# A hybrid conv/attention/MoE block: the last four experts with whole weight tiles, sums begun on top of x, and stores from two queues

## The chip, the cores and the metric

One core of a Trainium2 chip runs the whole block. The metric is the device time of one execution in microseconds; the kernel before took 550.88 us (median of three runs, 549.04 to 552.13).

## What is computed

For 512 tokens of width 1024 the block does, in float32, a modulated norm, a conv group and an attention group, an output projection, and then a mixture of 32 experts (one group of four, two experts in it per token). Only that last part matters here:

```python
y = jnp.zeros_like(h)
for e in range(N_EXPERTS):
    a = jax.nn.silu(h @ w_gate_e[e]) * (h @ w_up_e[e])
    y = y + gates[:, e:e + 1] * (a @ w_down_e[e])
...
return x + g_f[:, None] * y
```

Each expert has gate and up weights of 1024 x 256 and down weights of 256 x 1024, so 3 MB in float32; all 32 have to be read once, about 100 MB.

## The kernel before

**Units.** The experts are sorted by the number of their tokens and worked off in twelve *units*: `ORDER = "eeellsllsxss"` (L921). An "e" or "l" unit holds two experts with 64 token places each, an "s" unit four experts with 32 places each, the "x" unit one with 64 and one or two pieces of 32. `PIECES` (L1011) gives the places as (first column, columns, expert). The last unit, number 11, is an "s" unit: four pieces of 32.

**Weights.** An expert's weights come as three tiles of 1 MB: part 0 and part 1 (half of the gate and half of the up rows each, two transfers of 512 KB) and "d" (down, one transfer of 1 MB). `load` (L979) takes a free place from the list `room` and returns the transfers; `loads_upto` (L1032) issues them from SP in the order of `keys`, all part 0 of a unit, then part 1, then "d". For the last unit `LAST` (L1029) changes this: its tiles are cut in two halves each, two experts at a time for parts 0 and 1 and all four at a time for "d", so that `load_keys` (L1004) issues all first halves before all second halves. The halves of "d" are column halves, 0 to 511 and 512 to 1023, as the two halves of the output are needed.

**A unit's work.** `gate_up` (L1471) multiplies the gathered tokens with gate and up (float32 products of the form 32 or 64 columns by 512; each shows as two TensorE instructions in the trace). ACT takes silu (L1483), DVE multiplies (L1485), `turn` (L1488) transposes the result on TensorE and ACT copies it to `aT` (L1494). `down` (L1496) makes, for each output half, a product per piece and per contraction half c (L1506), then DVE scales by the gate (L1509, `yf`), ACT rounds it to a first part in float32r (L1510), and POOL subtracts that to get the rest (L1511; DVE in the last unit). `one_hot` (L1460) makes on DVE the matrix that puts the rows of a unit at their tokens. `combine` (L1514) multiplies by it, for each output half and each of four blocks of 128 tokens (tt), two float32r products (L1523) into a PSUM bank, and DVE adds the bank to the rows of x in SBUF (L1526). For the last unit, `store=True`, SP then stores the 256 KB piece (L1528).

**Order.** The order of instructions on TensorE, DVE, ACT, POOL and SP is that of the program; nothing is moved by a scheduler. At the last unit (L1573 to L1589) TensorE does: the rest of the sums of the units before, `down` of unit 10, the first half of `gate_up` of unit 11, the sums of unit 10 (paced by two banks `fb` and DVE's adds), the second half of `gate_up`, `turn`, and then

```python
down, comb = cur.down(dve), combine([cur], (fb, fb, tr, tr), True)
for hf in range(2):
    run(down, 1)
    run(comb, 4)
```

so half 0 of `down`, its four sums and stores, then half 1 of `down`, its four sums and stores. PSUM has eight banks: four `acc`, two `fb`, two `tr`. After it, each engine reads the number of overflowing units (L1640) and jumps over the code for them (L1643), which is not run with these inputs.

Of the kernel before, what the change touches and what calls it, by code (L numbers as in the profile page):

```python
# [12 lines left out]
F32 = mybir.dt.float32  # L13
# [28 lines left out]
def hybrid_block(ctx: ExitStack, tc: tile.TileContext, A, out, dbg=None, stop=None):  # L42
# [52 lines left out]
    def S(shape, dt=F32):  # L95
        return slots.tile(shape, dt, tag="s", name=nm("s"))
# [49 lines left out]
    def xrow(tt):  # L146
        return X[tt // 2][:, tt % 2, :]
# [831 lines left out]
    def load(key, n):  # L979

        e, part = key
        o = Wtile()
        o.room = room.pop(0)
        shape = [128, 2, 1024] if part == "d" else [128, 2, 4, 256]
        o.t = (W if o.room == "r" else S)(shape)
        if isinstance(e, int):
            pick = lambda w: w[e]
        else:
            if part == 0:
                reg_of[e] = sp.value_load(od[0:1, e[1]:e[1] + 1], min_val=0, max_val=31)  # L990
            pick = lambda w: w[bass.ds(reg_of[e], 1)].rearrange("e p a b -> (e p) a b")
        if part == "d":
            ds = [(o.t[:, :, cs], pick(wd)[:, :, cs]) for cs in cuts(1024, n)]
        else:
            ds = [(o.t[:, k, js], pick(w)[:, 4 * part + js.start:4 * part + js.stop, :])
                  for js in cuts(4, n) for k, w in ((0, wg), (1, wu))]
        Wt[key] = o
        per = len(ds) // n
        return [ds[i:i + per] for i in range(0, len(ds), per)]
# [1 line left out]
    def cuts(m, n):  # L1001
        return [slice(i, i + m // n) for i in range(0, m, m // n)]

    def load_keys(ks):  # L1004

        for ds in zip(*[load(key, min(len(ks), 2)) for key in ks]):
            for o, i in sum(ds, []):
                sp.dma_start(o, i)


    PIECES = {2: [(0, 64, 0), (64, 64, 1)], 4: [(32 * i, 32, i) for i in range(4)],  # L1011
              "x": [(0, 64, 0), (64, 32, 0), (96, 32, 1)], 1: [(0, 64, 0)]}
# [13 lines left out]
        keys += sum(ks if units else [ks[0], ks[2], ks[1]], [])  # L1026
        units.append((kind, *u_))
    nxt = [0]
    LAST = {(units[-1][2][0], "d"): 4}  # L1029
    LAST.update({(units[-1][2][i], part): 2 for i in (0, 2) for part in (0, 1)})  # L1030

    def loads_upto(n):  # L1032
        while room and nxt[0] < min(n, len(keys)):
            m = LAST.get(keys[nxt[0]], 1)
            if len(room) < m:
                break
            load_keys(keys[nxt[0]:nxt[0] + m])
            nxt[0] += m

    dve.scalar_tensor_tensor(G2, G2, 1.0, col("nf"), op0=OP.add, op1=OP.mult)  # L1040
    dve.scalar_tensor_tensor(G2n, G2n, 1.0, col("nfn"), op0=OP.add, op1=OP.mult)
# [399 lines left out]
    class Unit:  # L1441
# [51 lines left out]
            self.aT = T()  # L1493
            act.copy(self.aT[:, :2 * n], pt[:, :2 * n])  # L1494

        def down(self, eng=pool):  # L1496

            n = self.n
            self.yhl = S([128, 2, 1024], F32R)
            for hf in range(2):  # L1500
                hs = slice(512 * hf, 512 * hf + 512)
                o = acc()
                for c in range(2):
                    for o_, w_, i in self.pieces:
                        w = self.weights(i, "d")
                        pe.matmul(o[o_:o_ + w_, :], self.aT[:, n * c + o_:n * c + o_ + w_], w.t[:, c, hs],  # L1506
                                  start=(c == 0), stop=(c == 1), tile_position=(0, o_), skip_group_check=True)
                yf = T()
                dve.scalar_tensor_tensor(yf[:n], o[:n], self.gate, gf[:n, hs], op0=OP.mult, op1=OP.mult)  # L1509
                act.copy(self.yhl[:n, 0, hs], yf[:n])  # L1510
                eng.tensor_tensor(self.yhl[:n, 1, hs], yf[:n], self.yhl[:n, 0, hs].bitcast(F32), op=OP.subtract)  # L1511
                yield

    def combine(us, banks=None, store=False):  # L1514

        for u_ in us:
            u_.one_hot()
        for hf in range(2):
            for tt in range(4):
                o = banks[tt]() if banks else fb()  # L1520
                for m, u_ in enumerate(us):
                    for k in range(2):
                        pe.matmul(o, u_.ot[:u_.n, tt * 128:(tt + 1) * 128], u_.yhl[:u_.n, k, 512 * hf:512 * hf + 512],  # L1523
                                  start=(m == 0 and k == 0), stop=(m == len(us) - 1 and k == 1))
                xr = xrow(tt)[:, 512 * hf:512 * hf + 512]
                dve.tensor_tensor(xr, xr, o, op=OP.add)  # L1526
                if store:
                    sp.dma_start(out[0, tt * 128:(tt + 1) * 128, 512 * hf:512 * hf + 512], xr)  # L1528
                yield

    def table_rows(o, reg, n):

# [38 lines left out]
    for n_ in range(len(units)):  # L1571
        last = n_ == len(units) - 1
        if last:  # L1573
            run(comb)
            run(prev.down())
            comb = combine([prev])
        cur.gate_up(lambda: last and run(comb))
        if n_ == 1:
            run(gate)
        nxt_u = start(n_ + 1)  # L1580
        if nxt_u:
            nxt_u.complete()
        if last:
            cur.turn()
            down, comb = cur.down(dve), combine([cur], (fb, fb, tr, tr), True)
            for hf in range(2):
                run(down, 1)
                run(comb, 4)
            break  # L1589
        if prev:  # L1590
            run(prev.down())
            done.append(prev)
        cur.turn()
        if len(done) == 2:
            comb, done = combine(done), []
        run(comb, 4)
        if n_ > 1:
            run(side, 1)
        r_ = [Wt[e, part].room for part in (0, 1) for e in units[n_][2]]
        if n_ < 3:  # L1600
            r_.remove("s")
        if n_:
            r_ += [Wt[e, "d"].room for e in units[n_ - 1][2]]
        room += r_
        loads_upto(len(keys))
        prev, cur = cur, nxt_u
# [4 lines left out]
    def over_body(k):  # L1611
        if k == 0:
            scatter()
        reg = sp.value_load(oi[0:1, k:k + 1], min_val=0, max_val=31)
        Wo = {}
        for part in (0, 1, "d"):
            o = Wtile()
            o.t = W([128, 2, 1024] if part == "d" else [128, 2, 4, 256])
            pick = lambda w: w[bass.ds(reg, 1)].rearrange("e p a b -> (e p) a b")
            if part == "d":  # L1620
                sp.dma_start(o.t, pick(wd))
            else:
                js = slice(4 * part, 4 * part + 4)
                sp.dma_start(o.t[:, 0], pick(wg)[:, js, :])
                sp.dma_start(o.t[:, 1], pick(wu)[:, js, :])
            Wo[part] = o
        ot_ = small(2, tag="ovt", bufs=2)
        oix = small(1, I32, tag="ovi", bufs=2)
        table_rows(ot_[:64], pool.value_load(oi[0:1, NOVER + k:NOVER + k + 1], min_val=0, max_val=NROW - 64), 64)
        dve.tensor_copy(oix[:64], ot_[:64, 0:1])  # L1630
        buf = gb[:, 0, :]
        gather(oix[:64], buf[:64], 64)
        u_ = Unit(1, ot_[:64, 0:1], ot_[:64, 1:2], buf, lambda i, part: Wo[part])
        u_.complete()
        u_.gate_up()
        u_.turn()
        run(u_.down())
        run(combine([u_]))

    n_over = nc.values_load(oi[0:1, 2 * NOVER:2 * NOVER + 1], min_val=0, max_val=NOVER)  # L1640
# [87 lines left out]
```

## Time and profile before

| | |
|---|---|
| median of three runs | 550.88 us |
| the profiled execution: device time | 550.6 us |
| its span, first to last instruction | 549.0 us |
| TensorE busy, DVE busy | 89%, 54% of the span |
| granted TensorE clock, mean | 0.968 |
| moved by DMA | 153.00 MB, 279 GB/s over the span |

In the rows further down, times are microseconds from the span's start, or nanoseconds where they say so; PE is TensorE's matmul, PEld its weight load, SPq and ACTq are the instructions that an engine's sequencer handles itself, such as the issue of a transfer. "out<-in" names tiles: `acc`, `f`, `tr` are PSUM banks, `s`, `w` the places of weights and of x, `t` the temporary tiles. A form such as 128*32 128x512 is a product with 32 stationary columns and 512 moving ones.

### The profile page before, as it was taken

The page shows a single profiled execution, that of the slowest core. Times are in us where ns is not written, and L with a number is a line of the kernel's source. Part 1 is how long each engine was busy: PE and PEld are TensorE (multiplying, and loading weights), DVE is VectorE, ACT ScalarE, POOL GpSimd, SP SyncE. Part 2 cuts the span into 40 slices and gives each one's busy share as a digit, 9 for nine tenths or more (in the row PEclk, how much of TensorE's full clock was granted, in tenths as well). Part 3 has the DMA queues.
Part 4 walks back from the last instruction along what each step waited for, and adds up shares of the span by engine and source line. Part 5 has one row for each costly group of instructions (what it writes and reads, how often), then busy time and mean ns, then how long its engine had stood idle before and what let it go on. Part 6 is the DMA issues. An engine that isn't in the chain of part 4 may idle for free.

```text
span 549.0 us, 8137 instructions
## 1 busy us (share of the span) xinstructions
PE 486.6 (89%) x2827; PEld 277.8 (51%) x2827; DVE 298.5 (54%) x631; ACT 197.3 (36%) x419; POOL 169.2 (31%) x147
## 2 busy tenths in 40 slices
PE   4999999948988979999998999999999789989962
PEld 3778865534643446688884443443434332424321
DVE  2447699998998676662456333436433231415532
ACT  4233754534578556752443513112221020211000
POOL 3110674975889563110000213112221120101100
PEclk9999999968999889999999989999999989999988
DMA  8999536935971234266959889999999999999972
GB/s 249 299 347 304 182 131 257 381 113 179 231 217 67 78 93 149 78 236 213 367 180 382 291 346 335 347 409 413 373 414 408 410 411 415 408 410 303 327 296 96
DMA packets 60946, 153.00 MB, mean 279 GB/s; under 512 B 7485, under 2 KB 27085, under 8 KB 55264
## 3 DMA queue, kind: packets, MB, share of 16 engines
q1 hardware_dynamic: 57712, 145.91, 74.7%
q0 software_dynamic: 1792, 3.97, 2.1%
q10 hardware_dynamic: 1392, 2.51, 1.3%
q8 instruction: 24, 0.39, 0.3%
q14 instruction: 26, 0.21, 0.1%
HBM read 149.84 MB, written 4.49 MB: 281 GB/s over the span
## 4 chain that ended last, share of the span: by engine, by line
PE 46%; DVE 23%; DMA 20%; ACT 3%; SPq 3%; issue 2%; POOL 1%; ACTq 0%; DVEq 0%; POOLq 0%
DVE dw L345 10%; PE acc L1480 10%; DMA s<-in_w_up_e_dram 9%; PE acc L1506 6%; PE f L1523 5%; DMA w<-in_w_up_e_dram 4%; PE acc L117 4%; PE acc L119 3%; PE acc L118 3%; DMA w<-in_w_down_e_dram 3%; DMA s<-in_w_down_e_dram 2%; DMA s<-in_w_ada_dram 2%; PE acc L909 2%; DVE sm L879 2%; PE acc L877 1%
## 5 line engine op out<-in xcount | busy, mean ns | idle before, releaser
L1480 PE MATMUL acc<-s,gw 128*32 128x512 f32 (+1 forms) x392 | 93.3, 604 | 1.5 <-DMA s<-in_w_up_e_dram 1.5
L117 PE MATMUL acc<-s,s 128*128 128x512 f32 (+3 forms) x160 | 64.8, 405 | 10.7 <-DVE s L318 8.2
L345 DVE SCALAR_TENSOR_TENSOR dw<-s,cwh,dw 128x512 f32<-128x512 f32 x60 | 63.6, 1061 | 1.5
L119 PE MATMUL acc<-s,s 128*128 128x512 f32 (+3 forms) x160 | 60.1, 376 | 1.4 <-DVE s L379 1.4
L118 PE MATMUL acc<-s,s 128*128 128x512 f32 (+3 forms) x160 | 60.1, 376 | 0.0
L1523 PE MATMUL f<-s,t 128*128 128x512 f32 x184 | 48.7, 412 | 10.8 <-DVE t L1462 8.1
L1480 PE MATMUL acc<-w,gw 128*32 128x512 f32 (+1 forms) x136 | 53.5, 619 | 4.1 <-DMA w<-in_w_up_e_dram 4.0
L1485 DVE TENSOR_TENSOR t<-t,acc 128x256 f32<-128x256 f32 x12 | 5.1, 421 | 91.0 <-ACT t L1483 91.0
L1511 POOL TENSOR_TENSOR s<-t,s 128x512 fp32r<-128x512 f32 x22 | 28.5, 1295 | 75.9 <-ACT s L1510 75.9
L1483 ACT ACTIVATE t<-acc 128x256 f32<-128x256 f32 x12 | 4.6, 384 | 127.8 <-PE acc L1480 127.8
L1480 PEld LDWEIGHTS acc<-s,gw 128*32 128x32 f32 (+1 forms) x392 | 25.8, 123 | 47.9 <-issue 46.4
L357 POOL TENSOR_TENSOR dw<-dw,s 128x512 f32<-128x512 f32 x30 | 45.6, 1518 | 13.1 <-ACT s L355 11.4
L1526 DVE TENSOR_TENSOR s<-s,f 128x512 f32<-128x512 f32 x52 | 35.2, 687 | 20.0 <-PE f L1523 20.0
L1506 PE MATMUL acc<-s,t 128*32 128x512 f32 (+1 forms) x200 | 45.3, 609 | 0.5 <-ACT t L1494 0.5
L1523 PEld LDWEIGHTS f<-s,t 128*128 128x128 f32 x184 | 31.1, 188 | 26.9 <-DVE s L1526 7.3
L1438 POOL DMA_INDIRECT s<-xg,sidx x11 | 11.2, 1020 | 106.9 <-PE tr L1454 65.5
L117 PEld LDWEIGHTS acc<-s,s 128*128 128x128 f32 x160 | 31.1, 194 | 25.2 <-DVE s L318 8.6
L1510 ACT CAST s<-t 128x512 fp32r<-128x512 f32 x24 | 14.8, 618 | 54.8 <-DVE t L1509 54.8
L119 PEld LDWEIGHTS acc<-s,s 128*128 128x128 f32 x160 | 31.1, 194 | 5.9 <-DVE s L379 1.8
L118 PEld LDWEIGHTS acc<-s,s 128*128 128x128 f32 x160 | 31.2, 195 | 3.4 <-issue 0.2
L1509 DVE SCALAR_TENSOR_TENSOR t<-acc,rt,gw 128x512 f32<-128x512 f32 x24 | 18.0, 751 | 27.0 <-PE acc L1506 27.0
L881 ACT ACTIVATE t<-acc,sm,qs 128x128 f32<-128x128 f32 (+3 forms) x32 | 19.7, 616 | 19.9 <-DVE sm L879 16.6
(313 smaller groups left out, 856.1 us busy)
## 6 DMA issues: line engine op xcount, KB each, us to landing
s<-in_w_down_e_dram SPq DMA_DIRECT2D x21, 1024.0 KB
s<-in_w_gate_e_dram SPq DMA_DIRECT2D x41, 512.0 KB
s<-in_w_up_e_dram SPq DMA_DIRECT2D x41, 512.0 KB
w<-in_w_ada_dram SPq DMA_DIRECT2D x16, 1024.0 KB
w<-in_w_gate_e_dram SPq DMA_DIRECT2D x15, 512.0 KB
w<-in_w_up_e_dram SPq DMA_DIRECT2D x15, 512.0 KB
w<-in_w_down_e_dram SPq DMA_DIRECT2D x7, 1024.0 KB
s<-in_w_ada_dram SPq DMA_DIRECT2D x6, 1024.0 KB
```

The costliest lines, as they stand in the source:

```text
L117: pe.matmul(o, lh, rh, start=start, stop=False)
L118: pe.matmul(o, lh, rl, start=False, stop=False)
L119: pe.matmul(o, ll, rh, start=False, stop=stop)
L345: dve.scalar_tensor_tensor(dw[:, t, :], u[:, t, k:k + 512], w, dw[:, t, :], op0=OP.mult, op1=OP.add)
L357: pool.tensor_tensor(dw[:, t, :], dw[:, t, :], z[(k - 1) % 2], op=OP.add)
L881: act.activation(e[:, :n], p[:, :n], AF.Exp, scale=qs[:, qt, h:h + 1], bias=H["nb"][:, qt:qt + 1], accum_out=H["rs"][:, qt:qt + 1])
L1480: pe.matmul(gu[sl, :], self.hg[:, j, sl], w.t[:, :, j % 4, :], start=(j == 0), stop=(j == 7), tile_position=(0, o_), skip_group_check=True)
L1506: pe.matmul(o[o_:o_ + w_, :], self.aT[:, n * c + o_:n * c + o_ + w_], w.t[:, c, hs], start=(c == 0), stop=(c == 1), tile_position=(0, o_), ...
L1509: dve.scalar_tensor_tensor(yf[:n], o[:n], self.gate, gf[:n, hs], op0=OP.mult, op1=OP.mult)
L1511: eng.tensor_tensor(self.yhl[:n, 1, hs], yf[:n], self.yhl[:n, 0, hs].bitcast(F32), op=OP.subtract)
L1523: pe.matmul(o, u_.ot[:u_.n, tt * 128:(tt + 1) * 128], u_.yhl[:u_.n, k, 512 * hf:512 * hf + 512], start=(m == 0 and k == 0), stop=(m == len ...
L1526: dve.tensor_tensor(xr, xr, o, op=OP.add)
```

## The change

1. The loads of the last unit: no more halves, two transfers of 512 KB for part 0 and 1 and one of 1 MB for "d", expert after expert, as in the other units. Only the very last tile ("d" of the fourth expert) comes in two column halves.
2. `down` takes both `acc` banks at its start and can work by groups of pieces. In the last unit it makes, for experts 0 and 1, both output halves, and then, for experts 2 and 3, half 0 (with DVE's scaling, ACT's rounding, and the subtraction on POOL) and half 1 (the subtraction on DVE).
3. `finish_last` replaces `down` and `combine` of the last unit. The one-hot matrix is made first. Then six of the eight sums are begun with x itself: a float32 product of the identity matrix and the rows of x, 128*128 128x512, into banks `fb`, `fb`, `tr`, `tr` for the four blocks of half 0 and `acc`, `acc` for blocks 0 and 1 of half 1. After `down` the two one-hot products go on top, and the bank is copied to SBUF: blocks 0 and 2 of half 0 on DVE, the other four on ACT. Blocks 2 and 3 of half 1 are done as before, in `fb` with DVE's add, ahead of blocks 0 and 1.
4. Stores are issued from SP and from ACT in turn.
5. `down` and `combine` are plain calls for the other units, with the same instructions in the same order.

```diff
-    LAST = {(units[-1][2][0], "d"): 4}
-    LAST.update({(units[-1][2][i], part): 2 for i in (0, 2) for part in (0, 1)})
+    LAST = units[-1][2][-1], "d"
     def loads_upto(n):
         while room and nxt[0] < min(n, len(keys)):
-            m = LAST.get(keys[nxt[0]], 1)
-            if len(room) < m:
-                break
-            load_keys(keys[nxt[0]:nxt[0] + m])
-            nxt[0] += m
+            key = keys[nxt[0]]
+            for o, i in sum(load(key, 2 if key == LAST else 1), []):
+                sp.dma_start(o, i)
+            nxt[0] += 1
...
-        def down(self, eng=pool):
+        def down(self, groups=None, first=None):
             n = self.n
             self.yhl = S([128, 2, 1024], F32R)
+            o = [acc(), acc()]
+
+            def products(hf, pieces):
+                for c in range(2):
+                    for o_, w_, i in pieces:
+                        w = self.weights(i, "d")
+                        pe.matmul(o[hf][o_:o_ + w_, :], self.aT[:, n * c + o_:n * c + o_ + w_], w.t[:, c, 512 * hf:512 * hf + 512],
+                                  start=(c == 0), stop=(c == 1), tile_position=(0, o_), skip_group_check=True)
+
+            groups = groups or [self.pieces]
+            for g in groups[:-1]:
+                for hf in range(2):
+                    products(hf, g)
             for hf in range(2):
                 hs = slice(512 * hf, 512 * hf + 512)
...
+                products(hf, groups[-1])
                 yf = T()
-                dve.scalar_tensor_tensor(yf[:n], o[:n], self.gate, gf[:n, hs], op0=OP.mult, op1=OP.mult)
+                dve.scalar_tensor_tensor(yf[:n], o[hf][:n], self.gate, gf[:n, hs], op0=OP.mult, op1=OP.mult)
                 act.copy(self.yhl[:n, 0, hs], yf[:n])
-                eng.tensor_tensor(self.yhl[:n, 1, hs], yf[:n], self.yhl[:n, 0, hs].bitcast(F32), op=OP.subtract)
-                yield
+                (dve if len(groups) > 1 and hf else pool).tensor_tensor(
+                    self.yhl[:n, 1, hs], yf[:n], self.yhl[:n, 0, hs].bitcast(F32), op=OP.subtract)
...
+    def finish_last(u_):
+
+        u_.one_hot()
+        o = {}
+        for tt, hf, bank in (0, 0, fb), (1, 0, fb), (2, 0, tr), (3, 0, tr), (0, 1, acc), (1, 1, acc):
+            o[tt, hf] = bank()
+            pe.matmul(o[tt, hf], ident, xrow(tt)[:, 512 * hf:512 * hf + 512], start=True, stop=False, skip_group_check=True)
+        u_.down([u_.pieces[:2], u_.pieces[2:]])
+        for hf, tts in (0, range(4)), (1, (2, 3, 0, 1)):
+            for n, tt in enumerate(tts):
+                xr = xrow(tt)[:, 512 * hf:512 * hf + 512]
+                known = (tt, hf) in o
+                if not known:
+                    o[tt, hf] = fb()
+                scattered(o[tt, hf], [u_], tt, hf, not known)
+                if not known:
+                    dve.tensor_tensor(xr, xr, o[tt, hf], op=OP.add)
+                elif hf or n % 2:
+                    act.copy(xr, o[tt, hf])
+                else:
+                    dve.tensor_copy(xr, o[tt, hf])
+                (act if n % 2 else sp).dma_start(out[0, tt * 128:(tt + 1) * 128, 512 * hf:512 * hf + 512], xr)
...
             cur.turn()
-            down, comb = cur.down(dve), combine([cur], (fb, fb, tr, tr), True)
-            for hf in range(2):
-                run(down, 1)
-                run(comb, 4)
+            finish_last(cur)
             break
```

`scattered` holds the two one-hot products of `combine` as they were.

## Rows read from the trace of the kernel before

**Rows 1.** The page, part 1: busy time of each engine.

```profile
PE 486.6 (89%) x2827; PEld 277.8 (51%) x2827; DVE 298.5 (54%) x631; ACT 197.3 (36%) x419; POOL 169.2 (31%) x147
```

**Rows 2.** The chain of waits in order of time, from 475 us: start, duration, what.

```profile
475.26 10.12 DMA w<-in_w_up_e_dram
...
520.27 3.64 PE acc L1480 x32
...
524.41 0.43 DVE t L1485
...
524.89 0.45 PE tr L1492 x2
...
525.78 1.97 PE acc L1506 x16
...
530.45 1.31 PE f L1523 x4
...
533.46 2.58 PE acc L1506 x16
...
538.32 0.52 PE f L1523
...
541.09 0.26 DVE s L1526
```

**Rows 3.** Waits from 470 us to the end: waiter, releaser, total, times, longest.

```profile
PE acc L1480 <- DMA w<-in_w_up_e_dram: 1.5, 1, 1.5
```

**Rows 4.** Stretches: length, busy time of PE, PEld, DVE, ACT, POOL, clock, DMA share, GB/s.

```profile
530.00:531.30 1.30, 0.85 (x4) 0.75 (x5) 0.41 (x2) 0.00 (x0) 0.00 (x0) 1.00 0.05 17
...
482.00:490.00 8.00, 6.48 (x52) 2.29 (x44) 0.38 (x1) 0.59 (x2) 0.00 (x0) 1.00 1.02 420
500.00:512.00 12.00, 12.00 (x75) 6.36 (x77) 7.16 (x11) 0.75 (x2) 2.10 (x2) 1.00 0.98 325
524.00:530.00 6.00, 2.36 (x18) 0.62 (x18) 1.96 (x4) 1.36 (x3) 0.00 (x0) 1.00 1.01 376
```

**Rows 5.** Timeline of PE at 285 us: L1236, float32, 128*128 128x512.

```profile
285.36 1.98 PE L1236 MATMUL acc<-s,rt 128*128 128x512 f32 x4
```

**Rows 6.** Timeline of PE in the "x" unit: two 32-column pieces, then 64 columns.

```profile
455.81 0.62 PE L1480 MATMUL acc<-w,gw 128*32 128x512 f32 x1
456.26 0.59 PE L1480 MATMUL acc<-s,gw 128*32 128x512 f32 x1
456.27 0.59 PE L1480 MATMUL acc<-w,gw 128*32 128x512 f32 x1
456.79 0.64 PE L1480 MATMUL acc<-s,gw 128*64 128x512 f32 x1
```

**Rows 7.** The granted clock of one stretch, columns as in rows 4.

```profile
531.34:534.76 3.42, 3.42 (x14) 1.49 (x16) 2.52 (x4) 0.00 (x0) 0.00 (x0) 0.50 0.58 214
```

**Rows 8.** Page, part 5: busy time and mean ns, idle time before; work on outputs.

```profile
L1511 POOL TENSOR_TENSOR s<-t,s 128x512 fp32r<-128x512 f32 x22 | 28.5, 1295 | 75.9 <-ACT s L1510 75.9
...
L1526 DVE TENSOR_TENSOR s<-s,f 128x512 f32<-128x512 f32 x52 | 35.2, 687 | 20.0 <-PE f L1523 20.0
...
L1510 ACT CAST s<-t 128x512 fp32r<-128x512 f32 x24 | 14.8, 618 | 54.8 <-DVE t L1509 54.8
...
L1509 DVE SCALAR_TENSOR_TENSOR t<-acc,rt,gw 128x512 f32<-128x512 f32 x24 | 18.0, 751 | 27.0 <-PE acc L1506 27.0
```

**Rows 9.** Single lines: count, ns shortest/median/longest, first and last start. PSUM to SBUF copies.

```profile
L1360 DVE COPY s<-acc x1: 691/691/691, 298.5 to 298.5; 128x512 f32<-128x512 f32 x1
...
L1359 ACT COPY s<-acc x1: 585/585/585, 297.6 to 297.6; 128x512 f32<-128x512 f32 x1
```

**Rows 10.** Single lines, same columns: issue of stores, and SP's next instruction.

```profile
L1528 SPq DMA_DIRECT2D out_dram<-s x8: 332/352/1465, 531.9 to 542.2; - x8
...
L1165 ACTq DMA_DIRECT2D xg<-t x8: 326/326/356, 268.6 to 295.0; - x8
...
L1640 SPq TENSOR_LOAD <-oi x1: 399/399/399, 543.1 to 543.1; - x1
```

More of the change, by code (lines that the diff above doesn't have):

```diff
@@ L1002, in cuts @@
         return [slice(i, i + m // n) for i in range(0, m, m // n)]
[L1004 to L1008, printed above, removed]
     PIECES = {2: [(0, 64, 0), (64, 64, 1)], 4: [(32 * i, 32, i) for i in range(4)],
@@ L1494, in turn, with scattered, combine @@
             act.copy(self.aT[:, :2 * n], pt[:, :2 * n])
-        def down(self, eng=pool):
+        def down(self, groups=None, first=None):
             n = self.n
             self.yhl = S([128, 2, 1024], F32R)
+            o = [acc(), acc()]
[9 more added lines that the diff above has]
+                    products(hf, g)
             for hf in range(2):
                 hs = slice(512 * hf, 512 * hf + 512)
[L1502 to L1507, printed above, removed]
+                products(hf, groups[-1])
                 yf = T()
-                dve.scalar_tensor_tensor(yf[:n], o[:n], self.gate, gf[:n, hs], op0=OP.mult, op1=OP.mult)
+                dve.scalar_tensor_tensor(yf[:n], o[hf][:n], self.gate, gf[:n, hs], op0=OP.mult, op1=OP.mult)
                 act.copy(self.yhl[:n, 0, hs], yf[:n])
-                eng.tensor_tensor(self.yhl[:n, 1, hs], yf[:n], self.yhl[:n, 0, hs].bitcast(F32), op=OP.subtract)
-                yield
-    def combine(us, banks=None, store=False):
+                (dve if len(groups) > 1 and hf else pool).tensor_tensor(
+                    self.yhl[:n, 1, hs], yf[:n], self.yhl[:n, 0, hs].bitcast(F32), op=OP.subtract)
+    def scattered(o, us, tt, hf, start=True):
+        for m, u_ in enumerate(us):
+            for k in range(2):
+                pe.matmul(o, u_.ot[:u_.n, tt * 128:(tt + 1) * 128], u_.yhl[:u_.n, k, 512 * hf:512 * hf + 512],
+                          start=(start and m == 0 and k == 0), stop=(m == len(us) - 1 and k == 1), skip_group_check=True)
+    def combine(us):
         for u_ in us:
@@ L1519, in combine @@
             for tt in range(4):
[L1520 to L1524, printed above, removed]
+                o = fb()
+                scattered(o, us, tt, hf)
                 xr = xrow(tt)[:, 512 * hf:512 * hf + 512]
                 dve.tensor_tensor(xr, xr, o, op=OP.add)
-                if store:
-                    sp.dma_start(out[0, tt * 128:(tt + 1) * 128, 512 * hf:512 * hf + 512], xr)
                 yield
+    def finish_last(u_):
[19 more added lines that the diff above has]
+                (act if n % 2 else sp).dma_start(out[0, tt * 128:(tt + 1) * 128, 512 * hf:512 * hf + 512], xr)
     def table_rows(o, reg, n):
@@ L1574, in hybrid_block @@
             run(comb)
-            run(prev.down())
+            prev.down()
             comb = combine([prev])
@@ L1584, in hybrid_block @@
             cur.turn()
-            down, comb = cur.down(dve), combine([cur], (fb, fb, tr, tr), True)
-            for hf in range(2):
-                run(down, 1)
-                run(comb, 4)
+            finish_last(cur)
             break
         if prev:
-            run(prev.down())
+            prev.down()
             done.append(prev)
@@ L1636, in over_body @@
         u_.turn()
-        run(u_.down())
+        u_.down()
         run(combine([u_]))
```

## The prediction

> **What bounds the kernel now.** The page's busy times come first: TensorE is busy for 89% of the span [rows 1], but that is a mean over stages, and the change touches only the last one. So the chain of waits in order of time is read next. Its last transfer is an up-weight tile of unit 10, waited for until 485.4 us; from there to the end the chain holds TensorE, DVE and ACT alone [rows 2]. The list of waits says the same: from 470 us on, products waited for a transfer once, 1.5 us, and that is the wait at 485 [rows 3]. So the weights of the last unit are not what is waited for, although they are still on their way. The stretches show how close they are: with whole tiles the queue moves 420 GB/s, with the 256 KB halves of the last unit 325 GB/s, with the halves of "d" 376 GB/s, and at 530 us it stops [rows 4]. From 524 to 530 us run some 2.26 MB; the last four 512 KB halves are 2.1 MB, so the first halves of "d" have landed at about 524.4 and the last part 1 tiles, 2.1 MB further back, at about 519. They are used at 525.78 and 520.27 [rows 2]. The transfers are 1.3 us ahead of TensorE. The reader is to see in the chain that what sets the end from 524 us on is a row of dependent steps, gone through twice: half of `down` (1.97, then 2.58 us), DVE, ACT, DVE, sums, stores.
>
> **The change part by part.** *Whole tiles.* 12.6 MB at 420 instead of 325 to 376 GB/s: begun at about 495 us, when unit 10's "d" tiles are in, they end at 495 + 30 = 525 instead of 530 us, the slow last tile included. TensorE does not wait for them before, so this gains nothing by itself; it only makes sure that "d" is there. Fewer issues on SP (21 instead of 40) gain nothing either, since SP waits for earlier transfers in any case.
>
> *Sums on top of x.* Six float32 products 128*128 128x512, two instructions each. The price of one: four such in a row take 1.98 us [rows 5], the last of them 0.6 to its end, so 0.46 between starts; the 32 of `gate_up`, four abreast and so eight steps, take 3.64 us [rows 2], 0.43 a step. I take 0.43, with 0.46 as the other end. Twelve make 5.2 us. They stand on TensorE's queue between `turn` (ends 524.89 + 0.45 = 525.34 [rows 2]) and `down`, which could start at 525.78. So 0.4 us of them lies beside ACT's copy and 4.7 us delays `down`. This is the dearest edit. It buys that six adds on DVE become plain copies, of which four go to ACT: 0.69 for DVE's add [rows 8] against 0.69 for a copy on DVE and 0.585 on ACT [rows 9].
>
> *`down` in two groups.* Before, four pieces of 32 columns ran abreast, four steps a half. Now two run abreast, twice as many steps: 4 halves of groups x 4 steps x 0.43 = 6.9 us instead of 3.4. That two of 32 run abreast is seen in the "x" unit [rows 6]. There a 64-column product waits at 456.79 until the pair begun at 456.27 is through (0.43 and 0.09), though it uses other columns; products of one size do overlap, as the four of `down`. Group 2 follows group 1 at one size, so I let its first step run beside group 1's last, 0.43 less; the other end is no overlap. The Trainium skill, "TensorEngine Tiling (Array Packing)", section Key Properties, says that different tiles run in parallel and that a change of the tiling mode drains the engine; by its rule both what rows 6 show and the overlap follow, and without the overlap the sum would be 0.4 us more.
>
> *The path.* Products with x until 530.5; group 1 until 533.9; half 0 of group 2 until 535.2, its last instruction ends at 535.4; half 1 at 537.1. Half 0 then takes DVE 0.75, ACT 0.62, POOL 1.30 [rows 8], so it is ready at 538.1, POOL's extra 0.6 us over DVE hidden half by half 1 of `down`. Half 1: 537.1 + 0.75 + 0.62 + 0.69 = 539.2 with the hops. The one-hot matrix, 0.4 us on the path before (between 529.9 and 530.45), is made while TensorE turns: gain 0.4, in the path above already. Then DVE's order counts: it does half 1's subtraction first and only then copies block 0 of half 0, until 539.95. That frees the bank for block 2 of half 1: two products to 540.6, add to 541.35, the second add (block 3) to 542.1. ACT's order counts too: the store of block 3 stands before its last two copies, waits for that add, is issued (0.33 [rows 10], and 0.1), and the copies end at 543.1 and 543.7. SP's last store goes out from 543.15 to 543.5, ACT's until 544.1. Before, the last add ended at 541.35 [rows 2], but SP's last store was issued at 542.2 and SP's next instruction began at 543.1 [rows 10], because two issues at the end took far longer than 0.35 us (the longest 1.47). From there to the end of the span 5.9 us pass, in SP's jump over the unused code and the closing of the program. They are kept, and the stores' landing lies inside them; ACT's store, 0.6 us later, has the same cover. So the span ends at 543.5 + 5.9 = 549.4, against 549.0.
>
> *Edits at nothing.* `down` and `combine` of the other units issue the same instructions in the same order. Both `acc` banks at the start of `down`: four banks, the last users are done by 524.8. Stores of half 0: issued at 532 to 534 before, beside work; now eight stores, 2 MB, fall into 539.8 to 544.1, and at the 0.32 to 0.42 MB a microsecond of rows 4 they land by 546 to 547, inside SP's 5.9 us. If that cover were gone they would cost up to 1 us.
>
> *The sum.* Against the steps of before: products with x +5.2, less the 0.4 that TensorE stood there; `down` 6.6 instead of 1.97 + 2.58, +2.0; the wait for half 0's DVE, ACT, DVE and one-hot (527.75 to 530.45) -2.7; half 0's sums between the halves (530.45 to 533.46) -3.0; from the end of `down` to the last copy that SP stores 6.0 instead of 5.3, +0.7; SP's slow issues (541.35 to 543.06, against 0.35) -1.4. Together +0.4 us. The profiled execution took 550.6 us (span 549.0, 1.6 around it), 0.3 below the median of 550.88; the median plus 0.4 is 551.3.
>
> **The clock.** From 531.34 to 534.76 the granted clock is 0.50, 1.2 GHz [rows 7], after TensorE had stood for 2.7 us; half 1 of `down` takes 2.58 instead of 1.97 us there [rows 2], the sums before it some 0.6 more. In my path TensorE is busy from 525 to 537, so I take 2.4 GHz throughout. The Trainium skill, "TensorE: Matmul & The Clock Gate", section Part 1, says that the throttled clock is the default and that activity lifts it; by its rule the fall goes, as in my sum, and were it to stay it would cost 1.7 us.
>
> **The rivals.**
> (a) *The transfers set the pace after all.* In ordinary runs they may be a little later than in this profile, only 1.3 us lie between, and TensorE would wait for the halves. Then ending 5 us earlier brings the stage forward by up to 4.4 us: 546.5. Against it: the list of waits has no such wait, and the new order puts 5.2 us of products ahead of `down`, which takes back such a gain.
> (b) *ACT stalls at its stores.* On SP one issue took 1.47 us instead of 0.33 [rows 10]. ACT has three issues ahead of its last two copies, and they would hold the copies, where SP's held nothing but stores. Stalls of 1.13 us at all three, less 1.0 us that ACT waits anyway for block 3, give +2.4: 553.7, slower. It decides from two stalls on. Against it: ACT's eight earlier stores took 0.33 to 0.36 each.
> (c) *The clock falls in `down` as before*: 3.4 us at half speed, +1.7: 553.0.
> (d) *The second queue takes away the tail's slow issues and the copies are in time*: 541.5 + 0.35 + 5.9, a span of 547.8, 549.6 for the median. For it: half of the stores leave SP. Against it: the last copies come later than the last add did.
> That the change doesn't do what it says can't be excluded for one part: products with x may wait for banks. Their last users are done by 521 (`fb`) and 525.74 (`tr`), so I give it nothing of its own.
>
> **How the numbers follow.** Half a percent, 2.75 us, is about what a measurement of this kernel can tell from no change; the three runs alone lie 3.1 us apart. The forecast has 0.58, (a) 0.10, (b) 0.14, (c) 0.08, (d) 0.10. All of (a) lies below 548.1, and 0.03 of the rest: faster 0.13. About 0.10 of (b), 0.03 of (c) and 0.05 of the forecast (no overlap, 0.46 a step, stores not covered, together 1.8 us, and noise) lie above 553.6: slower 0.18. The same 0.69. The range leaves out (a), and above it part of (b): 549.0 to 554.0.
>
> **What would show it.** Right: no wait of TensorE for transfers after 485 us; twelve instructions of some 0.43 us each between `turn` and `down`; loads at an end by 525 us; `down` over at about 537; the last copy on ACT at 543 to 544; a full clock from 525 to 540. Wrong: TensorE waiting for "d" tiles; products with x at a quarter or twice the price; store issues of over 1 us on ACT; an end more than 6.5 us after SP's last store.

## The result, and the profile after

The kernel after takes 553.04 us (median of 20 runs, 549.7 to 556.49) against 551.28 us before (20 runs, 546.95 to 553.31): ratio 1.0051 [1.003, 1.0072]. It is slower by half a percent, some 1.8 us. 551.3 was forecast, with no change as the likeliest case, at 0.69, and slower at 0.18. The value lies inside the range, but the kernel is clearly slower, and that was not the forecast.

The profiled execution has a span of 551.2 us, against 549.0 of before. First TensorE's order in the last unit, in the trace's timeline of after: start, duration, engine, line, operation, and in brackets how long the engine had stood and for what.

```profile
525.20 0.44 PE L1484 MATMUL tr<-ident,t 128*128 128x128 f32 x2 [1.04 <-DVE t L1477]
525.48 1.88 PE L1539 MATMUL f<-s,ident 128*128 128x512 f32 x4
...
530.72 0.62 PE L1498 MATMUL acc<-s,t 128*32 128x512 f32 x1
...
532.47 0.59 PE L1498 MATMUL acc<-w,t 128*32 128x512 f32 x1
532.48 1.01 PE L1498 MATMUL acc<-s,t 128*32 128x512 f32 x3
...
533.79 2.31 PE L1498 MATMUL acc<-s,t 128*32 128x512 f32 x10
...
537.36 0.96 PE L1518 MATMUL f<-s,t 128*128 128x512 f32 x3 [0.83 <-POOL s L1511]
```

The unit's `turn` starts at 525.20, 0.3 us later than before [rows 2]. The twelve instructions of the products with x follow it without a gap until `down` starts at 530.72. `down` steps every 0.43 us with two pieces abreast; from 532.47 on four are abreast, since half 0 of group 2 has joined half 1 of group 1. It is through at 536.1. Then one-hot products wait once for POOL, 0.83 us.

The engines that end the work, from the timelines of DVE, ACT and POOL of the same kernel:

```profile
536.04 1.27 POOL L1511 TENSOR_TENSOR s<-t,s 128x512 fp32r<-128x512 f32 x1 [21.89 <-ACT s L1510]
```
```profile
537.66 0.69 DVE L1511 TENSOR_TENSOR s<-t,s 128x512 fp32r<-128x512 f32 x1 [0.69 <-ACT s L1510]
538.27 0.68 DVE L1553 COPY s<-f 128x512 f32<-128x512 f32 x1
538.87 0.68 DVE L1553 COPY s<-tr 128x512 f32<-128x512 f32 x1
539.77 1.28 DVE L1549 TENSOR_TENSOR s<-s,f 128x512 f32<-128x512 f32 x2 [0.22 <-PE f L1518]
```
```profile
541.47 1.07 ACT L1551 COPY s<-acc 128x512 f32<-128x512 f32 x2 [1.49 <-PE acc L1518]
542.57 1.20 ACTq L1554 DMA_DIRECT2D out_dram<-s  x1
```

The last two copies on ACT are over at 542.54. Its last store takes 1.20 us to issue, and then ACT too has to go through the jump over the unused code. SP's four stores, in the view of line 1554 (shortest, median and longest in ns; first and last start in us):

```profile
L1554 SPq DMA_DIRECT2D out_dram<-s x4: 332/348/358, 539.0 to 542.1; - x4
```

None of SP's issues is slow any more; before, one took 1465 ns [rows 10]. So SP's last store is issued by 542.41, where before it was 543.06. Counted from the start of `turn`, 17.20 us instead of 18.18: up to here the change gains 1.0 us in these two profiles. What comes behind on SP takes the gain and more. Three views of after show it: SP's read of the register at L1662 (L1640 before, 399 ns [rows 10]), the wait at its jump, and the closing code.

```profile
L1662 SPq TENSOR_LOAD <-oi x1: 911/911/911, 542.5 to 542.5; - x1
```
```profile
SPq L1665 <- SPq L1665: 4.0, 1, 4.0
```
```profile
L1746 SPq EVENT_SEMAPHORE  x14: 17/28/28, 548.4 to 551.2; - x14
```

The jump and the closing code of before:

```profile
SPq L1643 <- SPq L1643: 2.8, 1, 2.8
```
```profile
L1724 SPq EVENT_SEMAPHORE  x14: 17/28/28, 547.4 to 548.9; - x14
```

The register read is 0.51 us longer, the jump 1.17 us (3.97 against 2.80), and the closing's fourteen semaphore instructions stretch over 2.7 instead of 1.5 us, because SP stands for 1.15 us in the middle of them. The read, the jump and the stand make 2.83 of the 2.89 us by which the stretch from SP's last store to the end has grown, 8.82 against 5.93. Less the 1.0 us won ahead of it, that is +1.9 us from `turn` to the end, about the difference of the medians.

Stretches of after, TensorE's clock and GB/s last: the loads, and the window of rows 7.

```profile
500.00:512.00 12.00, 12.00 (x76) 6.47 (x78) 6.87 (x10) 0.73 (x2) 2.10 (x2) 1.00 1.03 410
...
525.00:526.00 1.00, 0.80 (x4) 0.56 (x5) 0.55 (x2) 0.32 (x1) 0.00 (x0) 1.00 0.13 47
```
```profile
531.34:534.76 3.42, 3.42 (x27) 1.04 (x24) 0.27 (x1) 0.00 (x0) 0.00 (x0) 1.00 0.00 0
```

Whole tiles run at 410 instead of 325 GB/s [rows 4] and are in shortly after 525 instead of 530 us; TensorE waits for a transfer once after 470 us, at 485 as before [rows 3]:

```profile
PE acc L1472 <- DMA w<-in_w_up_e_dram: 1.6, 1, 1.6
```

The granted clock is 1.00 where it was 0.50 [rows 7].

### The profile page after: what moved, and what is told of

It reads as the page before. It is cut to its first block, busy times and chain, and to the rows that moved or that the text cites. A ratio compares the mean times of both kernels' runs of the same rounds, so it can differ in the third digit from the quotient of the medians.

```text
span 551.2 us, 8095 instructions
## 1 busy us (share of the span) xinstructions
PE 492.4 (89%) x2839; PEld 279.7 (51%) x2839; DVE 294.7 (53%) x626; ACT 199.2 (36%) x423; POOL 170.5 (31%) x148
## 3 DMA queue, kind: packets, MB, share of 16 engines
q0 software_dynamic: 1792, 3.97, 2.2%
## 5 line engine op out<-in xcount | busy, mean ns | idle before, releaser
L1511 POOL TENSOR_TENSOR s<-t,s 128x512 fp32r<-128x512 f32 x23 | 29.7, 1293 | 98.7 <-ACT s L1510 88.8
L1530 DVE TENSOR_TENSOR s<-s,f 128x512 f32<-128x512 f32 x48 | 32.6, 687 | 18.6 <-PE f L1518 18.6
```

Of the source, the lines that this page charges most:

```text
L1511: (dve if len(groups) > 1 and hf else pool).tensor_tensor(self.yhl[:n, 1, hs], yf[:n], self.yhl[:n, 0, hs].bitcast(F32), op=OP.subtract)
```

## The experiments

The theory to be tested: SP's tail, from its last store to the end, grew, not the engines' work. Three causes could be behind it. The stores: more of them, from two queues, are in flight when SP jumps. ACT: it now stores last and jumps at the same moment as SP. The place of the closing code: SP's program has another length, so another piece of it has to be fetched at the end. The rival to all three: the engines' new order or the whole tiles cost the time, and the tail is chance. Another is that SP simply waits for the last store to land.

One execution varies by 1.8 us (standard deviation of the twenty runs of before, and of after), so totals tell 2 us apart with difficulty; the profiles are therefore cut at two places, the start of the last unit's `turn` and the end of SP's last store issue, and the pieces compared. All in us, from one profile of each: "rest" is from the end of SP's last store issue to the end of the span, "read" SP's register read, "jump" the time from SP's branch to its next instruction, "ACT's jump" when it starts against SP's, and "stop" a stand of over 1 us between two instructions of the closing code.

| | ratio to before [95%] | turn to SP's last store | rest | read | jump | ACT's jump | stop | turn to end |
|---|---|---|---|---|---|---|---|---|
| before | | 18.18 | 5.93 | 0.40 | 2.80 | -6.4 | none | 24.11 |
| after | 1.0051 [1.003, 1.0072] | 17.20 | 8.82 | 0.91 | 3.97 | +0.95 | 1.15 | 26.02 |
| after, again (k) | 1.0031 [0.9998, 1.0064] | 17.25 | 8.83 | 0.93 | 3.90 | +0.63 | 1.22 | 26.08 |
| a | 1.0035 [1.0003, 1.0068] | 18.07 | 7.90 | 0.43 | 2.75 | -6.3 | 1.98 | 25.97 |
| b | 1.0059 [1.0018, 1.0101] | 19.71 | 5.96 | 0.60 | 2.62 | -8.1 | none | 25.67 |
| c | 1.0002 [0.9961, 1.0043] | 17.23 | 7.80 | 0.29 | 3.58 | +0.60 | 1.13 | 25.03 |
| d | 1.0029 [0.9997, 1.006] | 15.44 | 8.57 | 0.91 | 3.75 | +0.82 | 1.13 | 24.01 |
| f | 1.0000 [0.9964, 1.0037] | 17.20 | 7.56 | 0.93 | 3.90 | +0.84 | none | 24.77 |
| g | 1.0012 [0.9981, 1.0044] | 16.41 | 6.36 | 0.57 | 3.05 | -6.4 | none | 22.77 |
| h | 1.0024 [0.9998, 1.0051] | 19.31 | 6.38 | 0.54 | 3.11 | -3.1 | none | 25.69 |
| j | 1.0018 [0.999, 1.0046] | 17.45 | 6.10 | 0.62 | 2.75 | -5.9 | none | 23.56 |
| i | 0.9908 [0.9871, 0.9945] | 12.44 | 5.58 | 0.28 | 2.56 | -2.5 | none | 18.02 |
| i, again (l) | 0.9922 [0.9886, 0.9958] | 12.44 | 6.41 | 0.29 | 3.39 | -2.5 | none | 18.85 |
| m | 0.9922 [0.9884, 0.996] | 12.97 | 5.94 | 0.28 | 2.92 | -7.6 | none | 18.91 |

**a: whole tiles alone.** The kernel before with after's load code.

```diff
-    LAST = {(units[-1][2][0], "d"): 4}
-    LAST.update({(units[-1][2][i], part): 2 for i in (0, 2) for part in (0, 1)})
+    LAST = units[-1][2][-1], "d"
```

> The kernel before with the change's loads alone (whole tiles, the very last in two halves); the work on the engines, the sums and the stores stay as before. Theory 1 (the transfers were never waited for; the loss of the change is its tail, where all eight stores are in flight while the engines jump to the closing code): loads end at 525 instead of 530 us, the span stays within 1 us of before (549.0), ratio 1.000 within 0.003, and from SP's last store issue to the end of the span about 5.9 us as before. Theory 2 (the tail is longer because SP's code is shorter and lies elsewhere): from SP's last store issue to the end 7.5 us or more, time +1.5 to +2.5 us. Rival (a) of the prediction (transfers set the pace): 2 to 4 us faster.

It ran 1.0035 [1.0003, 1.0068], and not by its engines: from `turn` to SP's last store it needs 18.07 us, as before. But its closing code stops too, for 1.98 us, earlier than in after: here behind the fifth of the 26 instructions that the trace shows after SP's jump, in after behind the thirteenth. The first nine of them, which took 0.6 us after, take 2.6:

```profile
L1641 SPq EVENT_SEMAPHORE  x9: 17/17/17, 550.6 to 553.2; - x9
```

This speaks for the third cause: on the engines nothing changed, and SP's program has other loads and another length.

**b: late stores.** The kernel before; half 0's four stores are held back and issued behind those of half 1.

```diff
-                    sp.dma_start(out[0, tt * 128:(tt + 1) * 128, 512 * hf:512 * hf + 512], xr)
+                    late.append((out[0, tt * 128:(tt + 1) * 128, 512 * hf:512 * hf + 512], xr))
+                    for o_, x_ in (late[-1:] if hf else []) + (late[:4] if hf and tt == 3 else []):
+                        sp.dma_start(o_, x_)
```

> The kernel before, with the four stores of half 0 held back on SP's queue until the four of half 1 are issued; nothing else moves. The engines' work must end as before, at 541.3 us. SP issues four more stores at the end, at 0.35 to 0.6 us each: last issue 1.5 to 2.5 us later than before. Theory 1 (stores in flight delay the code of the jump): from SP's last issue to the end of the span 8 us or more instead of 5.9, so the span is 4 to 5 us longer. Theory 2 (place of the code): 5.9 us as before, the span only 1.5 to 2.5 us longer.

All eight stores now go out between 539.4 and 544.5 us, and the read, the jump and the closing stay short:

```profile
SPq L1647 <- SPq L1647: 2.6, 1, 2.6
```

The kernel is slower; its last issue comes 1.5 us later, and the rest behind it is 5.96, as before. Stores in flight didn't lengthen SP's tail here. Nor does SP wait for them to land: its first instruction behind the jump runs at 548.14, and the last store lands at 548.25. In a and in the second profile of after (k) it runs 0.17 and 0.13 us ahead of the last landing as well.

**c: half of the stores.** The kernel after, with a condition at the store.

```diff
+                if hf:
-                (act if n % 2 else sp).dma_start(...)
+                    (act if n % 2 else sp).dma_start(...)
```

> The changed kernel without the four stores of half 0 (columns 0 to 511 of the output are left out). The engines' work stays as in the changed kernel, but SP and ACT issue two stores each. Theory 1: from SP's last store issue to the end about 6 us instead of 8.8, the span 548 to 549 us, 2 to 3 us below the changed kernel and no longer than before. Theory 2: from SP's last issue to the end 8 us or more still, time within 1 us of the changed kernel.

With only four stores the jump is still 3.58 and the stop still there, 1.13; the read alone falls to 0.29. So the number of stores in flight doesn't make the jump long either; the read may depend on it. The times, 1.0002, are those of before, as if the stores had been the cause; the profile has 25.03 us from `turn` to the end, 1.0 less than after, 0.6 of it the read. SP's program is two stores shorter, and the stop has moved from behind the thirteenth of the closing instructions to behind the seventeenth.

**d: one group.** The kernel after, all four pieces abreast in `down`.

```diff
-        u_.down([u_.pieces[:2], u_.pieces[2:]])
+        u_.down([[], u_.pieces])
```

> The changed kernel with all four experts of the last unit in one group, four abreast, both halves of down one after the other; products with x, copies and stores as in the change. In the change down took 5.4 us (530.7 to 536.1), since half 1 of group 1 and half 0 of group 2 ran abreast; in one group it should take 3.5, half 0 ready 1.9 us earlier and half 1 1.9 us earlier. All theories of the tail: the whole end shifts, stores and all, span 549.3, 1.9 us below the changed kernel. If the loads were what group 2 waits for, nothing is gained (they end at 525 us, so I don't expect it).

`down` takes eight steps instead of twelve, from 531.33 to 534.9. SP's last store is issued 1.8 us sooner after `turn` than in after (15.44 against 17.20): this is what the groups cost. The tail is that of after. As no product waits for "d", nothing stands against that price. The times, 1.0029, don't tell it from after.

**f: another place.** The kernel after with 28 more stores in code that SP jumps over. They are never executed; the closing code only stands further on in SP's program.

```diff
-                    sp.dma_start(out[0, tt * 128:(tt + 1) * 128, :], xrow(tt))
+                    for cs in cuts(1024, 8):
+                        sp.dma_start(out[0, tt * 128:(tt + 1) * 128, cs], xrow(tt)[:, cs])
```

> The changed kernel with 28 more store instructions in SP's code that is jumped over (the whole rows stored in eighths), so that SP's closing code lies 29 instructions further on; nothing that is executed differs. In the changed kernel SP stands for 1.15 us between the 13th and the 14th of its 27 closing instructions, in the kernel with the loads alone, whose SP code is 8 instructions longer, for 1.98 us between the 5th and the 6th: the same place in the code. Theory 2 (place of SP's code): that stop is gone, the span 1.1 us shorter than the changed kernel's, some 550.1. Theory 1 (stores in flight), already unlikely: nothing changes.

To SP's last store it is the kernel after to the hundredth, 17.20. The stop is gone, the jump is as long as before it:

```profile
SPq L1665 <- SPq L1665: 3.9, 1, 3.9
```
```profile
L1747 SPq EVENT_SEMAPHORE  x14: 17/28/28, 549.4 to 551.0; - x14
```

Fourteen semaphore instructions in 1.6 us again, from `turn` to the end 24.77 instead of 26.02: 1.25 us less, nearly all of it the stop. The ratio of its runs is 1.0000 [0.9964, 1.0037]; the intervals of after overlap with it, so that it is the profiles that show the gain.

**g: the same for a.** The load change alone, with the same skipped stores.

> The kernel before with the change's loads alone and the same 28 instructions in SP's skipped code. Theory 2: the stop of 1.98 us in the closing code is gone, from SP's last store issue to the end 5.9 us as before, and the ratio to the kernel before is 1.000 within 0.003: whole tiles by themselves cost and gain nothing. If the loads themselves cost something, the ratio stays at 1.003 to 1.004 and the engines' work before the closing code is longer.

No stop, ratio 1.0012 [0.9981, 1.0044]. Within that interval the whole tiles neither cost nor gain anything.

That g needs only 16.41 us to SP's last store is the clock. TensorE stands as long as before, 2.74 us, but here the granted clock doesn't fall behind it, in the window that corresponds to that of rows 7:

```profile
531.32 1.17 PE L1521 MATMUL f<-s,t 128*128 128x512 f32 x4 [2.74 <-DVE t L1460]
```
```profile
532.21:535.63 3.42, 3.07 (x22) 1.06 (x20) 2.52 (x5) 0.00 (x0) 0.00 (x0) 1.00 0.60 223
```

DVE's last add ends 14.88 us after the start of `turn`; in before, a, b and j, where the clock falls to 0.50 (1.2 GHz), it is 16.43 to 16.46. So the same work takes 1.6 us more or less with the clock. Against g, the 17.20 us of after are not 1.0 us gained but 0.8 lost.

**h: one queue.** f, with all eight stores on SP.

```diff
-                (act if n % 2 else sp).dma_start(...)
+                sp.dma_start(...)
```

> The changed kernel with the 28 skipped instructions and all eight stores from SP. Compared with the kernel that has the skipped instructions and both queues. Theory 4 (the jump of SP takes 4.0 us instead of 2.8 because ACT, which now copies and stores to the very end, jumps in the same microsecond, or because two queues of stores are ahead of the code): with one queue SP's jump takes 2.8 to 3.2 us; SP's last issue comes 0.5 to 1 us later, since it has all eight; the span within 0.7 us. If the jump stays at 4 us, the second queue is not what lengthens it.

ACT is done early and jumps 3.1 us before SP. The read is 0.54, the jump 3.11, the rest 6.38 instead of 7.56: 1.2 us less. But the issues of SP are slow again, in the view of its stores:

```profile
L1554 SPq DMA_DIRECT2D out_dram<-s x8: 355/418/1444, 537.0 to 542.1; - x8
```

Its last store is issued 19.31 us after `turn`, 2.1 us later than in f, and not 0.5 to 1 us as expected. By the profiles the second queue gains 2.1 us ahead of the tail and gives 1.2 back in it; by the times the two kernels can't be told apart. Of the 1.2 us, the jump's 0.8 is no more than what two profiles of one kernel differ by (i and l, 2.56 and 3.39).

**i: what the readings point to.** Skipped stores as in f, whole tiles, one group, no product with x ahead of `down`. Only two sums are begun with x, in gaps of TensorE behind `down`, and they are ACT's, copy and store; DVE adds the other six, and SP stores them.

```diff
...
+        u_.down([[], u_.pieces])
+        begin(3, 0, tr)
+        end(3, 0)
+        end(0, 0, fb)
+        end(1, 0, fb)
+        end(2, 0, tr)
+        begin(0, 1, acc)
+        end(0, 1)
+        end(1, 1, acc)
+        end(2, 1, fb)
+        end(3, 1, fb)
...
```

`begin` makes the product with x; `end` makes the one-hot products, then the copy or the add, and the store.

> A version meant to beat both: whole tiles, one group of four abreast, both halves of down one after the other, and only two of the eight sums begun on x, each put where TensorE stands or has time (after down, and between the sums of the halves); ACT copies and stores these two, DVE adds the other six and SP stores them; SP's skipped code as in the two kernels above. From the rows of the change: turn ends at 525.4, down at 529.3, half 0's rest ready at 530.6 and half 1's at 531.6, eight sums of 0.46 us with one product of 0.86 between until 535, six adds of 0.69 us on DVE from 531.6 to 535.7, last store issued at 536.2; with 6 to 8 us behind it the span is 542 to 544.5 us, ratio 0.988 to 0.993 to the kernel before. If the stores in flight set the end (2 MB in 532 to 537.5) it is no worse than 545.

0.9908 [0.9871, 0.9945], faster than both kernels. The timelines of TensorE and DVE, first and last rows of the stage:

```profile
525.26 0.62 PE L1498 MATMUL acc<-s,t 128*32 128x512 f32 x1 [0.46 <-ACT t L1486]
...
528.31 0.60 PE L1498 MATMUL acc<-s,t 128*32 128x512 f32 x2
528.84 1.12 PE L1540 MATMUL tr<-s,ident 128*128 128x512 f32 x2
```
```profile
527.26 0.75 DVE L1509 SCALAR_TENSOR_TENSOR t<-acc,rt,gw 128x512 f32<-128x512 f32 x1 [2.55 <-PE acc L1498]
...
534.45 1.28 DVE L1551 TENSOR_TENSOR s<-s,f 128x512 f32<-128x512 f32 x2
```

Both halves of `down` run in one go from 525.26 to 528.8; they start 0.9 us behind the start of `turn`, where after starts them 5.5 us behind it. DVE's last add ends at 535.73, where before it ended at 541.35 [rows 2]. The read is 0.28, the jump 2.56, the rest 5.58.

**j, k, l, m.** The kernel before with 81 more SP instructions among those skipped, the kernel after word for word, i word for word, and i without any product with x.

> The kernel before with 81 more instructions in SP's skipped code (the whole rows stored once more in sixteenths), so that the place where the changed kernel stops lies behind the 14th of SP's closing instructions; nothing that is executed differs. Theory 2 (place of SP's code): SP stands there for 1 to 2 us, where the kernel before stood nowhere; the span 1 to 2 us longer for the same work, ratio 1.002 to 1.004. If the stop has to do with the change's loads or stores: no stop, ratio 1.000.

> The changed kernel once more, word for word, beside the others on one chip. Ratio 1.003 to 1.007 as on record; the same stop of 1.1 us in SP's closing code and a jump of SP of about 4 us, so that the rest behind SP's last store is again 8.8 us within 0.5.

> The version meant to beat both once more, beside the version without sums on x: ratio 0.987 to 0.995, span 6 to 7 us below the kernel before when the stages ahead of the last unit take the same time.

> That version without any sum on x: all eight sums added on DVE, all eight stores from SP. TensorE is 1.7 us shorter, but DVE has 8 x 0.69 us instead of 6 behind 531.6: the last add 1.4 us later, at 537.1, the last store of SP with it; ACT is done early, so SP's jump takes 2.6 to 3 us as in that version. If sums on x pay where TensorE has time: 1 to 1.5 us longer than that version. If they don't: the same within 0.5 us.

k repeats after: 17.25, 8.83, a jump of 3.90, a stop of 1.22. What the profile of after showed was no chance of one execution. l repeats i at 0.9922 [0.9886, 0.9958]. Its span is 4.8 us below before's, and not 6 to 7 as expected. Its jump is longer than i's, 3.39 against 2.56, though ACT jumps as early, so 0.8 us of SP's jump come and go in one and the same kernel. m gives the same ratio as l with no product with x at all: DVE does two adds, 1.1 us, more and waits 0.8 us less. j is a miss. The program was lengthened so that a stop should fall behind the fourteenth closing instruction, and there is none; its rest is 6.10. That place is not the one at which the others stop, but 128 instructions further on; that the stop would come again after 128 was a guess.

## Why the prediction was wrong

**The step that failed** is "From there to the end of the span 5.9 us pass, in SP's jump over the unused code and the closing of the program. They are kept". They are 8.82 (8.83 in k). The list of what would prove it wrong names it: "an end more than 6.5 us after SP's last store". The prediction kept 5.93 us because nothing in that code was edited. But its length changed with what surrounds it:

- *The stop, 1.15 us.* Shown by f, which differs from after by code that never runs and loses the stop and little else; g does the same to a. SP's program as built has 1252 instructions after (in k and d too), 1248 in c and 1260 in a, and the stop falls behind the 13th, the 17th and the 5th of the 26 that the traces show after the jump: behind the 1238th or 1239th of the program each time. In the nine profiles without a stop the program has 1281 to 1379, and that place lies in skipped code. What SP stands for is not shown. The trace has fetches of instructions, on a queue of its own kind; the view of DMA from 548 to 550 us of after lists two 8 KB packets, which start at 548.28 and 548.50, just ahead of the stop (548.66 to 549.80), and nothing else:

```profile
q14 instruction: 2, 0.02, 2.8%
```

  f has two such packets in its closing code as well, and stands nowhere. What j adds is that a place 128 instructions further on was met without a stop; whether the stop comes again at another step stays open.
- *The jump, +1.17 us.* In five profiles ACT starts its jump 0.6 to 1.0 us behind SP's, and SP's takes 3.58 to 3.97. In nine ACT starts its own 2.5 us or more ahead of SP, and SP's takes 2.56 to 3.39. The branches of after, SP's and ACT's:

```profile
L1665 SPq COMPARE_BRANCH  x1: 53/53/53, 543.7 to 543.7; - x1
```
```profile
L1665 ACTq COMPARE_BRANCH  x1: 54/54/54, 544.7 to 544.7; - x1
```

  ACT's own jump goes the same way: 3.2 to 3.7 us in the five, 3.2 and 3.3 in i and l, where DVE jumps 0.7 us behind ACT, and 2.4 to 2.7 in the other seven. b and c speak against the number of stores in flight: eight late stores with 2.62, four with 3.58. h changes only who stores, and goes from 3.90 to 3.11, which alone is within what i and l differ by. That the code of engines that jump together comes through the same fetch is the likely reading, not a shown one. The Trainium skill, "Runtime: NRT & Kernel Launch", section Instruction fetch mechanics, says that a taken branch to code outside the pages held forces a fetch before the engine goes on, and that block boundaries are mostly hidden. The jumps agree with the first: the branch itself takes 53 ns, and 2.56 to 3.97 us pass behind it. On the second, if the stop is such a boundary, 1.13 to 1.98 us of it were not hidden.
- *The read, +0.51 us.* It is 0.91 to 0.93 in the four profiles in which both queues issue all eight stores, 0.28 to 0.62 in the others. Why is open.

**The engines' path** came out better than forecast: SP's last issue ends at 542.41 instead of 543.5, though the stage began 0.3 us later. By its terms:

- *Products with x, +5.2 us until 530.5.* `down` starts at 530.72, 0.3 us of it the later start. Right. That they are the dearest edit fits d and i: where they go (and two of them return behind `down`), SP's last store comes 3.0 us sooner after `turn`, though i has another order of sums and stores, too.
- *`down` 6.6 us, over at 537.1.* It took 5.4 us, over at 536.1. The mechanism was right and the size too small: one step was allowed to overlap, but all four steps of half 0 of group 2 run beside half 1 of group 1. The Trainium skill, "TensorEngine Tiling (Array Packing)", section Key Properties, has tiles work independently; the row at 532.48 agrees, and the sum by its rule alone, twelve steps of 0.43 or 5.2 us, would have been the better one.
- *Half 0 ready at 538.1, last copy at 543.7.* POOL is through at 537.31, ACT's last copy at 542.54, 0.8 and 1.2 us earlier, about what `down` gained.
- *SP's slow issues gone, -1.4.* Right: none above 0.36 us after (0.44 in k); one returns when SP stores alone (h, 1.44).
- *ACT's last store, "the same cover".* It took 1.20 instead of 0.33 us. That issue costs nothing itself, since k, where it took 0.58, has the same rest; that ACT, busy to the end, jumps with SP was not seen.
- *Whole tiles at nothing, loads over at 525.* Right (g: 1.0012 [0.9981, 1.0044]).
- *The clock at 2.4 GHz throughout.* Right, 1.00 in the window of rows 7 and from 525 to 541 us; rival (c) is out. But the fall that this takes away isn't in every execution of the kernel before, as g shows.

Of the rivals, (a) is out: no wait for a transfer went or came. (b) has its stall, but at the one store with nothing behind it but ACT's own jump. (d) named the slow issues that went. With 5.9 us behind SP's last store the span would have been 548.3, 0.7 below before's. That the time lies inside the range all the same is luck: the end of SP's last store came 1.1 us sooner than forecast, and the stretch behind it was 2.9 us longer.

## What to carry to other kernels

An edit that takes time off the engines pays only if the end of the program follows. So compare the stretch behind the last store as well, down to jump and closing code. Where a total moves by half a percent, time the same kernel with unused instructions added before the edit is blamed. Letting the engines that aren't needed for the end finish and jump early went with the shorter jumps here; that it is the cause isn't shown. Work that replaces an add behind a product should stand in a gap of TensorE behind the critical product, never ahead of it: six sums ahead delayed `down` by 4.6 us, and two behind it gained half a microsecond to SP's last store (12.44 against 12.97) and nothing in the times.

## What was not expected of the hardware

Code that never runs can change the time by its length alone: 28 unused stores took 1.25 us off the end of f. A jump over unused code took SP 2.56 to 3.97 us in fourteen profiles, the longest where ACT jumped right behind it. The issue of a 256 KB store, 0.33 to 0.36 us as a rule, takes up to 1.66 us near the end: the sixth of eight where SP stores all (1.21 to 1.66 in before, a, g, h and j), and the last of an engine in others (SP 1.05 in i, ACT 1.20 after); two queues don't always remove this. And after the same stand of 2.74 us TensorE's granted clock fell to 0.50 in before and stayed at 1.00 in g. Of the best kernel's gain, the part of each edit (both banks at once, the one-hot matrix made early, the full clock through `down`) wasn't measured one by one.
